# Fixing where VectorE's feed-forward weight sums stand in its queue (two-layer decoder trunk, one core)

## The chip, the cores and the metric

One core of a Trainium2 chip runs the whole program. The time is the device time of one execution in microseconds (us); the time before is 2376.92 us, the median of 3 runs (2371.43 to 2380.17). All instruction times below are read from one profiled execution of the kernel before.

## The reference, cut to what matters

The model is a trunk of two residual layers on 1024 tokens of width 1024. Layer 0 mixes with retention and RWKV-7 heads, layer 1 with sliding-window attention; each is followed by a SwiGLU feed-forward network of width 2816. The change is in the feed-forward networks only:

```python
def swiglu(h, w_gate, w_up, w_down):
    return (jax.nn.silu(h @ w_gate) * (h @ w_up)) @ w_down
...
    h = h + mix
    n = rms_norm(h, norm2_g[layer])
    h = h + swiglu(n, ffn_w_gate[layer], ffn_w_up[layer], ffn_w_down[layer])
return rms_norm(h, final_g)
```

## The kernel before, in words

**Arithmetic.** Activations are kept transposed (128 channels by tokens), the tokens in two halves of 512; `h[0]` and `h[1]` hold the residual of each half in SBUF. A float32 factor is split into a high and a low part, and a product is three matmuls of 128x128 by 128x512 (hi·hi, hi·lo, lo·hi). `prod` (L1172) issues them at L1175, L1176, L1177, so a product over 4 contraction tiles is 12 matmuls into one PSUM bank. The weight is split for each product by `wsplit` (L335 on ScalarE for the high part, L336 mostly on GpSimd for the low part) or by `vsplit` (L1348 and L1349). The split tiles rotate through six buffers.

**Products of blocks.** Instead of eight block products for a 2x2 block matrix, the feed-forward matrices use seven, with sums of weight blocks and of activation blocks (Winograd's form of Strassen's scheme). The weight sums are made on VectorE from weights just loaded, in place as far as possible:
- In the gate and up matrices: `wsums` (L1202) makes four sums (L1208 to L1211) of a pair's four 128x512 blocks; there is one call for gate and one for up. `late_splits` (L1256) is a generator that calls it for every pair of output tiles and loads the next pair's raw weights behind it.
- In the down matrix: `down` (L1378) makes s1 = a21 + a22, W0 = s1 - a11, then a21 = a11 - a21 and later W0 = a12 - W0, all through `vop`, so all have L1375.

**Gate and up.** First come the *early* products (`ffn_early`, L1240): all 11 pairs, two of seven products, each ended by `up` (L1226, VectorE), which multiplies silu(gate) by the up product straight out of PSUM. Then come the *late* pairs (`ffn_pair`, L1284; `late`, L1179): five products a matrix, whose additions into SBUF are L1182. The first late pair's weight sums are asked for before the last early pair, the second's while the first late pair's products are issued. The PSUM banks `ps_m` (two of them) are passed from the last early pair to the first late one: the late product that takes the bank has to wait until `up` has read it.

**Down.** The 11 tiles of the hidden dimension are worked through in groups: two groups of 4 in layer 0 (the rest is done in another way), groups of 4, 4 and 3 in layer 1. In a group there are four pairs of output tiles (`dp` 0 to 3), and for each step a loop over them. Call the banks A[dp] and B[dp]. The steps are: A = a11·X; B = W0·X2, with additions into h[1]; A += a12·X, with additions into h[0]; B += a21·X3, with additions into h[1]; B += a22·X4, with additions into h[0]; then A = s1·X1, each followed by an addition of A[dp] into h[1]; and last A += W0·X6 *into the same four banks*, each followed by a second addition of A[dp] into h[1]. TensorE may start the last step's product into A[dp] only when VectorE has read A[dp] for the first of these two additions. The next group's weights are loaded meanwhile, and nothing in the data ties the next group's sums to these additions.

**What sets the order.** The program is written as one stream; a scheduler, which runs over it with a timeline of its own, decides for each engine in which order its instructions stand. On the chip each engine works strictly in that order and waits on semaphores: an instruction whose operand isn't there holds up all behind it on its engine. `keep_in_program_order` (used by `keep`, L488, on DMAs) fixes some instructions; otherwise the scheduler is free within the data dependencies.

Of the kernel before, what the change touches and what calls it, by code (L numbers as in the profile page):

```python
# [13 lines left out]
ALU = mybir.AluOpType  # L14
# [190 lines left out]
class Kern:  # L205
# [281 lines left out]

    def keep(self, i):  # L488
        return self.tc.keep_in_program_order(i)

    def loads(self):

# [706 lines left out]
        use("12", u1)  # L1199
        yield  # L1200

    def wsums(self, raw, sp):  # L1202

        V = self.nc.vector
        f1, f2 = raw
        a11, a12, a21, a22 = f1[:, :HT], f1[:, HT:], f2[:, :HT], f2[:, HT:]
        s1 = self.t(sp, [P, HT], "ws", 2)
        V.tensor_tensor(out=s1, in0=a21, in1=a22, op=ALU.add)  # L1208
        V.tensor_tensor(out=a21, in0=a11, in1=a21, op=ALU.subtract)
        V.tensor_tensor(out=a11, in0=s1, in1=a11, op=ALU.subtract)  # L1210
        V.tensor_tensor(out=a12, in0=a12, in1=a11, op=ALU.subtract)  # L1211
        v = dict(s1=s1, s2=a11, s3=a21, s4=a12, a22=a22)
        return lambda nm: self.wsplit(v[nm], HT)

    def uses(self, L, p, sp, x=None):

        nc, sg = self.nc, {}
        V, S = nc.vector, nc.scalar

        def gate(nm, c):  # L1220
            sg[nm] = self.t(sp, [P, HT], "sg", 2) if nm == "11" else c
            S.activation(sg[nm], c, AF.Silu)

        def up(nm, c):
            o = x[nm] if x else sg[nm]
            V.tensor_tensor(out=o, in0=sg[nm], in1=c, op=ALU.mult)  # L1226
            d = self.hid[2 * L + int(nm[1]) - 1][2 * p + int(nm[0]) - 1]
            if x and p == NP - 1:
                self.owed.append((d, o))
            else:  # L1230
                nc.sync.dma_start(d, o)

        return gate, up
# [22 lines left out]
    def late_splits(self, L, wp):  # L1256

        def load(p):
            raws = [[self.rawtile(wp) for _ in range(2)] for _ in range(2)]
            for j in range(2):  # L1260
                for i, nm in enumerate(("gate", "up")):
                    self.nc.sync.dma_start(raws[i][j], self.A[f"w_{nm}{L}"][2 * p + j])
            return raws

        nxt = load(0)
        for p in range(NP):
            ws = [self.wsums(r, wp[0]) for r in nxt]
            if p == 0:
                yield
            if p + 1 < NP:  # L1270
                nxt = load(p + 1)
            for nm in ("s2", "s1", "s3", "a22", "s4"):
                for i in range(2):
                    yield ws[i](nm)
# [97 lines left out]
        return self.t(pool, [P, m * P], "ws", bufs)[:, : n * P].rearrange("p (k c) -> p k c", c=P)  # L1372

    def vop(self, o, x, y, f=ALU.add):
        self.nc.vector.tensor_tensor(out=o, in0=x, in1=y, op=f)  # L1375
        return o

    def down(self, L, fp, fz, rest, X=()):  # L1378


        op, S = self.vop, self.nc.scalar
        h0, h1 = (self.kt(self.h[hf]) for hf in range(2))
        dps = range(KT // 2)
        j = len(X)

        def place():
            nonlocal j
            i, j = j % (12 if L else 14), j + 1
            if i >= 8 if L else i < 6:
                return self.t(fp, [P, 2, HT], "ha", 4 if L else 6, F32R)  # L1390
            return self.t(self.pp, [P, 2, HT], "n8", 8, F32R)

        def plain(hf, f):
            return self.plain8(L, hf, f, place(), self.t(fp, [P, HT], "hr", 4))

        for gi, g in enumerate(DGROUPS[L]):
            n, ps = g[1] - g[0], range(*g)
            ta, tb = ("fffy", "mmrc")[:: 1 - 2 * (gi % 2)]
            s1, u0, a1 = [], [], []
            W = [self.wdown(L, 0, g, fp, "wd0", 5)]  # L1400
            X = X or [plain(0, 2 * p) for p in ps]
            W += [self.wdown(L, 2 * i, g, fp, "wd0", 5) for i in (1, 2, 3)]
            for i in dps:
                W[i] += self.wdown(L, 2 * i + 1, g, fp, "wd1", 6 - L)
            A = [self.pst(t, [P, HT]) for t in ta]
            for dp in dps:
                a11, a12, a21, a22 = W[dp]
                self.prod(A[dp], self.vsplit(a11), X, True, False)
                u0.append(self.t(fz, [P, HT], "u0", 4))
                S.copy(u0[dp], A[dp])  # L1410
                s1.append(op(self.wsum(fp, n, 4, 8), a21, a22))
                a1.append(a11)
                W[dp][0] = op(self.wsum(fp, n, 4, 8), s1[dp], a11, ALU.subtract)
            X = [self.sums8(L, p, 2, place()) for p in ps]
            B = [self.pst(t, [P, HT]) for t in tb]
            for dp in dps:
                self.prod(B[dp], self.vsplit(W[dp][0]), X, True, False)
                y = op(self.t(fz, [P, HT], "y", 2), B[dp], u0[dp])
                op(h1(2 * dp), h1(2 * dp), y)
                op(W[dp][2], a1[dp], W[dp][2], ALU.subtract)  # L1420
            X = [plain(0, 2 * p + 1) for p in ps]
            for dp in dps:
                self.prod(A[dp], self.vsplit(W[dp][1]), X, False, True)
                op(h0(2 * dp), h0(2 * dp), A[dp])
                op(W[dp][0], W[dp][1], W[dp][0], ALU.subtract)
            X = [self.sums8(L, p, 3, place()) for p in ps]
            for dp in dps:
                self.prod(B[dp], self.vsplit(W[dp][2]), X, False, False)
                y = op(self.t(fz, [P, HT], "y", 2), B[dp], u0[dp])
                op(h1(2 * dp + 1), h1(2 * dp + 1), y)  # L1430
            X = [self.sums8(L, p, 4, place()) for p in ps]
            while self.owed:
                self.keep(self.nc.sync.dma_start(*self.owed.pop(0)))
            for _ in rest:
                pass
            for dp in dps:
                self.prod(B[dp], self.vsplit(W[dp][3]), X, False, True)
                op(u0[dp], B[dp], u0[dp])
                op(h0(2 * dp + 1), h0(2 * dp + 1), u0[dp])
            X = [self.sums8(L, p, 1, place()) for p in ps]  # L1440
            X6 = [plain(1, 2 * p + 1) for p in ps]
            if g[1] == NP:
                yield
            A = [self.pst(t, [P, HT]) for t in ta]
            for dp in dps:
                self.prod(A[dp], self.vsplit(s1[dp]), X, True, False)
                op(h1(2 * dp + 1), h1(2 * dp + 1), A[dp])
            for dp in dps:
                self.prod(A[dp], self.vsplit(W[dp][0]), X6, False, True)
                op(h1(2 * dp), h1(2 * dp), A[dp])  # L1450
            X = ()
        yield

# [387 lines left out]
```

## Time and profile before

| | us |
|---|---|
| median of 3 runs (lowest, highest) | 2376.92 (2371.43, 2380.17) |
| the profiled execution, whole | 2374.81 |
| its span, first to last instruction | 2373.0 |
| VectorE (DVE) busy in the span | 1667.4 (70%) |
| ScalarE (ACT) busy | 1054.7 (44%) |
| GpSimd (POOL) busy | 948.4 (40%) |
| mean granted clock of TensorE | 0.99 of full speed |

A row of the timeline gives start, duration, engine, line, operation, output<-inputs with shapes, and in brackets how long the engine sat idle before and what released it. PE is TensorE's matmuls, each shown 0.39 us long though the next may start earlier; "PEclk" is the granted share of its clock. Names of tiles are the program's, without numbers: `ws` a weight sum, `wd` a raw down weight, `wq` and some `n` raw gate and up weights, `w` and `wr` split weights, `h` the residual, `ps_..` PSUM banks, `nq` temporaries.

### The profile page before, as it was taken

The numbers are of one execution on the slowest core, as the hardware profiler recorded it, in microseconds if no ns is written. First come the engines' busy times: TensorE is split into PE (matmuls) and PEld (weight loads), VectorE is DVE, ScalarE is ACT, GpSimd is POOL, SyncE is SP. The second block draws the span as 40 slices with busy tenths as digits, with TensorE's granted clock in tenths as the row PEclk, the third lists the DMA queues.
The fourth block names the chain that finished last, engine by engine and source line by source line (L and its number), as shares of the span: only waits on it lengthen the run. The fifth ranks groups of instructions, "written<-read, shape, count | busy, mean of one in ns | idle before, by whom it ended". The sixth has DMA issues, their size and how long they took to land. (4 is left out here: it accounts for less than half of the span.)

```text
span 2373.0 us, 35626 instructions
## 1 busy us (share of the span) xinstructions
PE 2312.1 (97%) x13092; PEld 1828.9 (77%) x13092; DVE 1667.4 (70%) x2630; ACT 1054.7 (44%) x1946; POOL 948.4 (40%) x746
## 2 busy tenths in 40 slices
PE   8999999999999999999999999999999999999997
PEld 6777777777777888888778877777787888877885
DVE  6876865774667358887675668567548778888776
ACT  5354533324456333333333556557645333333335
POOL 3123221201342057776667300002103577767665
PEclk9999999999999999999999999999999999999998
DMA  7555544443445545554554321232236465547652
GB/s 271 203 199 197 176 154 132 128 115 114 148 164 183 208 164 206 211 197 163 218 220 142 123 66 64 71 127 71 100 128 221 170 216 213 209 175 280 245 193 87
DMA packets 167741, 395.92 MB, mean 167 GB/s; under 512 B 42896, under 2 KB 45584, under 8 KB 167568
## 3 DMA queue, kind: packets, MB, share of 16 engines
q1 hardware_dynamic: 164448, 388.15, 47.8%
q10 hardware_dynamic: 2832, 4.45, 0.5%
q8 instruction: 104, 1.70, 0.3%
q0 software_dynamic: 288, 1.05, 0.1%
q14 instruction: 69, 0.57, 0.1%
HBM read 271.29 MB, written 116.92 MB: 164 GB/s over the span
## 5 line engine op out<-in xcount | busy, mean ns | idle before, releaser
L240 PE MATMUL ps_f<-n,w 128*128 128x512 f32 x1440 | 385.6, 415 | 8.6 <-ACT w L335 6.4
L240 PEld LDWEIGHTS ps_f<-n,w 128*128 128x128 f32 x1440 | 268.2, 192 | 93.6 <-issue 24.5
L335 ACT CAST w<-wr 128x512 fp32r<-128x512 f32 x244 | 147.9, 612 | 182.9 <-PE ps_f L352 73.1
L336 POOL TENSOR_TENSOR w<-wr,w 128x512 fp32r<-128x512 f32 x68 | 92.1, 1363 | 280.0 <-ACT w L335 223.0
L336 DVE TENSOR_TENSOR w<-wr,w 128x512 fp32r<-128x512 f32 (+1 forms) x176 | 123.8, 706 | 71.5 <-ACT w L335 71.3
L336 POOL TENSOR_TENSOR w<-wq,w 128x512 fp32r<-128x512 f32 x92 | 130.5, 1431 | 29.2 <-ACT w L335 27.2
L351 PE MATMUL ps_f<-n,w 128*128 128x512 f32 x356 | 141.7, 398 | 0.0
L352 PE MATMUL ps_f<-n,w 128*128 128x512 f32 x356 | 141.0, 396 | 0.6 <-POOL w L336 0.6
L350 PE MATMUL ps_f<-n,w 128*128 128x512 f32 x356 | 140.8, 396 | 0.6 <-ACT n L1601 0.5
L1182 DVE TENSOR_TENSOR nq<-ps_m,u 128x512 f32<-128x512 f32 x88 | 58.8, 685 | 104.3 <-PE ps_m L1177 104.2
L336 POOL TENSOR_TENSOR wx<-wr,wx 128x512 fp32r<-128x512 f32 x8 | 10.6, 1319 | 301.8 <-ACT wx L335 301.6
L1175 PE MATMUL ps_f<-n,w 128*128 128x512 f32 x298 | 118.5, 398 | 4.7 <-DVE h L1375 3.1
L1175 PE MATMUL ps_m<-n,w 128*128 128x512 f32 x300 | 117.5, 392 | 1.5 <-DVE h L1375 1.5
L1176 PE MATMUL ps_f<-n,w 128*128 128x512 f32 x298 | 117.2, 393 | 0.1
L1176 PE MATMUL ps_m<-n,w 128*128 128x512 f32 x300 | 116.8, 389 | 0.0
L1177 PE MATMUL ps_m<-n,w 128*128 128x512 f32 x300 | 116.8, 389 | 0.0
L1177 PE MATMUL ps_f<-n,w 128*128 128x512 f32 x298 | 116.7, 393 | 0.0
L358 POOL TENSOR_TENSOR n<-nq,n 128x512 fp32r<-128x512 f32 x54 | 91.5, 1707 | 8.9 <-ACT n L356 8.9
L1175 PE MATMUL ps_m<-cb,w 128*128 128x512 f32 x240 | 93.4, 389 | 1.0 <-DVE nq L1182 1.0
L1176 PE MATMUL ps_m<-cb,w 128*128 128x512 f32 x240 | 93.4, 389 | 0.0
L1177 PE MATMUL ps_m<-cb,w 128*128 128x512 f32 x240 | 93.4, 389 | 0.0
L1349 POOL TENSOR_TENSOR w<-wd,w 128x512 fp32r<-128x512 f32 (+1 forms) x53 | 76.0, 1444 | 34.8 <-ACT w L1348 34.8
(525 smaller groups left out, 6467.1 us busy)
## 6 DMA issues: line engine op xcount, KB each, us to landing
hc<-n SPq DMA_DIRECT2D x74, 512.0 KB, 2.6
wsp<-w SPq DMA_DIRECT2D x54, 512.0 KB, 3.3
w<-wsp SPq DMA_DIRECT2D x54, 512.0 KB, 3.4
wq<-in_w_gate SPq DMA_DIRECT2D x44, 512.0 KB, 4.3
u<-u SPq DMA_DIRECT2D x88, 256.0 KB, 2.9
n<-hc SPq DMA_DIRECT2D x43, 512.0 KB, 5.5
wr<-in_w_in SPq DMA_DIRECT2D x34, 512.0 KB, 4.8
hid<-n SPq DMA_DIRECT2D x66, 256.0 KB, 2.0
```

What stands on the lines that cost most here:

```text
L240: self.nc.tensor.matmul(out, lhsT, rhs, **kw)
L335: nc.scalar.copy(hi[:, :n], raw[:, c])
L336: self.lo.tensor_tensor(out=lo[:, :n], in0=raw[:, c], in1=hi.bitcast(F32)[:, :n], op=ALU.subtract)
L350: nc.tensor.matmul(ps, hi, rh, start=k == 0, stop=False)
L351: nc.tensor.matmul(ps, hi, rl, start=False, stop=False)
L352: nc.tensor.matmul(ps, lo, rh, start=False, stop=k == n - 1)
L358: e.tensor_tensor(out=lo, in0=src, in1=hi.bitcast(F32), op=ALU.subtract)
L1175: mm(ps, hi, xh, start=first and k == 0, stop=False, skip_group_check=True)
L1176: mm(ps, hi, xl, start=False, stop=False, skip_group_check=True)
L1177: mm(ps, lo, xh, start=False, stop=last and k == len(w) - 1, skip_group_check=True)
L1182: add = lambda o, x, y: V.tensor_tensor(out=o, in0=x, in1=y, op=ALU.add)
L1349: nc.gpsimd.tensor_tensor(out=lo, in0=v, in1=hi.bitcast(F32), op=ALU.subtract)
```

## The change

A helper `behind(i, first)` tells the scheduler that instruction i stands behind instruction `first`. It is an edge for ordering only (NoSync): both are on VectorE, and no semaphore is added.
- In `down`, group g+1's s1[dp] = a21 + a22 stands behind group g's *second* addition of A[dp] into h[1] (the list `ends`). W0 and the in-place difference follow by their data.
- In `late_splits`, for the second late pair the first two sums of gate and of up stand behind the last early pair's multiplication `up`.

```diff
+    def behind(self, i, first):
+        self.tc.add_manual_dep(
+            i.ins, first.ins.name,
+            mybir.DependencyInfo(mybir.DependencyClass.NoSync, mybir.DependencyReason.DATA), reason="behind",
+        )
...
-    def wsums(self, raw, sp):
+    def wsums(self, raw, sp, first=None):
...
-        V.tensor_tensor(out=s1, in0=a21, in1=a22, op=ALU.add)
-        V.tensor_tensor(out=a21, in0=a11, in1=a21, op=ALU.subtract)
+        i = [V.tensor_tensor(out=s1, in0=a21, in1=a22, op=ALU.add)]
+        i.append(V.tensor_tensor(out=a21, in0=a11, in1=a21, op=ALU.subtract))
+        if first is not None:
+            for x in i:
+                self.behind(x, first)
...
-            ws = [self.wsums(r, wp[0]) for r in nxt]
+            ws = [self.wsums(r, wp[0], last if p == 1 else None) for r in nxt]
             if p == 0:
                 yield
+                last = self.last_up
...
                 s1.append(op(self.wsum(fp, n, 4, 8), a21, a22))
+                if ends:
+                    self.behind(self.last_vop, ends[dp])
...
+            ends = []
             for dp in dps:
                 self.prod(A[dp], self.vsplit(W[dp][0]), X6, False, True)
                 op(h1(2 * dp), h1(2 * dp), A[dp])
+                ends.append(self.last_vop)
```

(`last_up` and `last_vop` keep the instruction that `up` and `vop` issued last.) Every engine has the same instructions as before. VectorE's order differs in five places: the second late pair of both layers, and the down groups behind the first (one in layer 0, two in layer 1). TensorE's differs in two short places, ScalarE's in one; the orders of GpSimd and of the DMA queue are the same. Lines below 495 of the kernel before stand 7 to 15 lines further down in the changed kernel (`vop` L1375 is L1386, `late` L1182 is L1189, `wsums` L1208 to L1211 are L1215, L1216, L1220 and L1221, `up` L1226 is L1236).

**Layer 0, down, from the first group to the second (VectorE).** The rows follow the last addition into h[0] of the first group. `h1_..<-h1_..,ps_f_1653` is the addition of A[0] (ps_f_1653, 1654, 1655 and ps_y_1656 are A[0] to A[3] of the last two steps), `ws<-wd1` an s1, `ws<-ws,wd0` a W0, `wd1<-wd0,wd1` the in-place difference of the second group. Before:

```order
L1375 TENSOR_TENSOR ws_1687_11179<-wd1_1677_11150 128x512
L1375 TENSOR_TENSOR h1_1033_6865<-h1_1033_6865,ps_f_1653_10990 128x512
L1375 TENSOR_TENSOR ws_1688_11181<-ws_1687_11179,wd0_1665_11122 128x512
L1375 TENSOR_TENSOR wd1_1677_11150<-wd0_1665_11122,wd1_1677_11150 128x4x128
L1375 TENSOR_TENSOR ws_1691_11200<-wd1_1678_11152 128x512
L1375 TENSOR_TENSOR h1_1033_6865<-h1_1033_6865,ps_f_1654_10991 128x512
L1375 TENSOR_TENSOR ws_1692_11202<-ws_1691_11200,wd0_1674_11144 128x512
L1375 TENSOR_TENSOR ws_1695_11221<-wd1_1679_11154 128x512
L1375 TENSOR_TENSOR wd1_1678_11152<-wd0_1674_11144,wd1_1678_11152 128x4x128
L1375 TENSOR_TENSOR ws_1696_11223<-ws_1695_11221,wd0_1675_11146 128x512
L1375 TENSOR_TENSOR ws_1699_11242<-wd1_1680_11156 128x512
L1375 TENSOR_TENSOR wd1_1679_11154<-wd0_1675_11146,wd1_1679_11154 128x4x128
```

And now:

```order
L1386 TENSOR_TENSOR h1_1033_6865<-h1_1033_6865,ps_f_1653_10990 128x512
L1386 TENSOR_TENSOR h1_1033_6865<-h1_1033_6865,ps_f_1654_10991 128x512
L1386 TENSOR_TENSOR h1_1034_6866<-h1_1034_6866,ps_f_1655_10992 128x512
L1386 TENSOR_TENSOR h1_1034_6866<-h1_1034_6866,ps_y_1656_10993 128x512
L1386 TENSOR_TENSOR h1_1033_6865<-h1_1033_6865,ps_f_1653_10990 128x512
L1386 TENSOR_TENSOR ws_1687_11179<-wd1_1677_11150 128x512
L1386 TENSOR_TENSOR ws_1688_11181<-ws_1687_11179,wd0_1665_11122 128x512
L1386 TENSOR_TENSOR wd1_1677_11150<-wd0_1665_11122,wd1_1677_11150 128x4x128
L358 TENSOR_TENSOR n8_1719_11339<-hr_1720_11340,n8_1719_11339 128x512
L1386 TENSOR_TENSOR h1_1033_6865<-h1_1033_6865,ps_f_1654_10991 128x512
L1386 TENSOR_TENSOR ws_1691_11200<-wd1_1678_11152 128x512
L1386 TENSOR_TENSOR ws_1692_11202<-ws_1691_11200,wd0_1674_11144 128x512
```

Before, one sum stood ahead of the first addition, three between the first and the second, and six between the second and the third (the row behind the last one shown); now the four first additions stand together, and each pair's three sums behind its second addition.

**Layer 1, from the last early pair to the first late one (VectorE).** `sg` is the last early `up`, `wq5`, `wq4` and `n8` are the second late pair's raw weights (gate, then up), `nq<-ps_m_2576` and `nq<-ps_m_2578` are the first late pair's first additions for gate and up. Before:

```order
L1208 TENSOR_TENSOR ws_2596_16467<-wq5_2583_16349 128x512
L1209 TENSOR_TENSOR wq5_2583_16349<-wq4_2582_16348,wq5_2583_16349 128x512
L1210 TENSOR_TENSOR wq4_2582_16348<-ws_2596_16467,wq4_2582_16348 128x512
L1211 TENSOR_TENSOR wq4_2582_16348<-wq4_2582_16348 128x512
L1208 TENSOR_TENSOR ws_2597_16472<-n8_2573_16336 128x512
L1209 TENSOR_TENSOR n8_2573_16336<-n8_2572_16335,n8_2573_16336 128x512
L1226 TENSOR_TENSOR sg_2565_16311<-sg_2565_16311,ps_m_2564_16272 128x512
L1182 TENSOR_TENSOR nq_2580_16346<-ps_m_2576_16342,u0_2574_16338 128x512
L1210 TENSOR_TENSOR n8_2572_16335<-ws_2597_16472,n8_2572_16335 128x512
L1211 TENSOR_TENSOR n8_2572_16335<-n8_2572_16335 128x512
L1182 TENSOR_TENSOR nq_2589_16382<-ps_m_2578_16344,u0_2575_16340 128x512
```

And now:

```order
L1236 TENSOR_TENSOR sg_2565_16311<-sg_2565_16311,ps_m_2564_16272 128x512
L1215 TENSOR_TENSOR ws_2596_16467<-wq5_2583_16349 128x512
L1215 TENSOR_TENSOR ws_2597_16472<-n8_2573_16336 128x512
L1189 TENSOR_TENSOR nq_2580_16346<-ps_m_2576_16342,u0_2574_16338 128x512
L1216 TENSOR_TENSOR wq5_2583_16349<-wq4_2582_16348,wq5_2583_16349 128x512
L1216 TENSOR_TENSOR n8_2573_16336<-n8_2572_16335,n8_2573_16336 128x512
L1220 TENSOR_TENSOR wq4_2582_16348<-ws_2596_16467,wq4_2582_16348 128x512
L1220 TENSOR_TENSOR n8_2572_16335<-ws_2597_16472,n8_2572_16335 128x512
L1221 TENSOR_TENSOR wq4_2582_16348<-wq4_2582_16348 128x512
L1221 TENSOR_TENSOR n8_2572_16335<-n8_2572_16335 128x512
L1189 TENSOR_TENSOR nq_2589_16382<-ps_m_2578_16344,u0_2575_16340 128x512
```

`up` went from behind six of the eight sums to the front, and the up matrix's first addition (`nq_2589`) still stands behind all eight; between them gate's and up's sums now alternate.

On TensorE in the same place two matmuls of the product into ps_c, which stood ahead of the product into ps_m_2578 (the one that takes the bank from `up`), now stand behind it.

More of the change, by code (lines that the diff above doesn't have):

```diff
@@ L1225, in up @@
             o = x[nm] if x else sg[nm]
-            V.tensor_tensor(out=o, in0=sg[nm], in1=c, op=ALU.mult)
+            self.last_up = V.tensor_tensor(out=o, in0=sg[nm], in1=c, op=ALU.mult)
             d = self.hid[2 * L + int(nm[1]) - 1][2 * p + int(nm[0]) - 1]
@@ L1374, in vop @@
     def vop(self, o, x, y, f=ALU.add):
-        self.nc.vector.tensor_tensor(out=o, in0=x, in1=y, op=f)
+        self.last_vop = self.nc.vector.tensor_tensor(out=o, in0=x, in1=y, op=f)
         return o
@@ L1383, in down @@
         dps = range(KT // 2)
-        j = len(X)
+        j, ends = len(X), []
         def place():
```

## The prediction

> **What bounds the kernel now.** I read the page's busy line first, then who TensorE waits for, then the timeline of TensorE and of VectorE around those waits.
>
> ```profile
> PE 2312.1 (97%) x13092; PEld 1828.9 (77%) x13092; DVE 1667.4 (70%) x2630; ACT 1054.7 (44%) x1946; POOL 948.4 (40%) x746
> ```
>
> TensorE is the bound: the feed-forward stages are one stream of matmuls, and only a gap in that stream can be won or lost. The list of TensorE's waits (total, times, longest) names three that VectorE ends in the places of this change, one instance each:
>
> ```profile
> PE ps_f L1175 <- DVE h L1375: 3.1, 1, 3.1
> PE ps_m L1175 <- DVE sg L1226: 2.1, 1, 2.1
> PE ps_m L1175 <- DVE h L1375: 1.5, 1, 1.5
> ```
>
> Call them **B** (layer 0, first to second down group), **C** (layer 1, last early to first late pair) and **E** (layer 1, second to third down group). The other two edited places, **A** (layer 0, late pair) and **D** (layer 1, first to second down group), have no wait here. What VectorE does ahead of B:
>
> ```profile
> 1206.71 1.79 DVE L1375 TENSOR_TENSOR ws<-wd 128x512 f32<-128x512 f32 x1 [1.16 <-POOL w L1349]
> 1208.42 0.67 DVE L1375 TENSOR_TENSOR h<-h,ps_f 128x512 f32<-128x512 f32 x1
> ...
> 1219.94 0.68 DVE L1375 TENSOR_TENSOR h<-h,ps_f 128x512 f32<-128x512 f32 x1
> ...
> 1224.01 0.67 DVE L1375 TENSOR_TENSOR h<-h,ps_f 128x512 f32<-128x512 f32 x1
> ...
> 1236.08 0.69 DVE L1375 TENSOR_TENSOR ws<-wd,ws 128x512 f32<-128x512 f32 x1 [2.02 <-POOL wr L1349]
> 1241.74 0.69 DVE L1375 TENSOR_TENSOR y<-ps_f,u 128x512 f32<-128x512 f32 x1 [4.96 <-PE ps_f L1177]
> ```
>
> The third first-addition, for which TensorE waits, runs at 1219.94 because six sums of the next group stand between it and the second one. The sums are early: when all are done, at 1236.77, VectorE idles 4.96 us until the first product that uses one has ended. A sum with both inputs in SBUF takes 0.67 us or up to 1.8; an addition out of PSUM stays at 0.68.
>
> **The change, part by part.** *B.* TensorE's rows at the wait:
>
> ```profile
> 1217.27 0.39 PE L1177 MATMUL ps_f<-n,w 128*128 128x512 f32 x1
> 1220.76 0.47 PE L1175 MATMUL ps_f<-n,w 128*128 128x512 f32 x1 [3.10 <-DVE h L1375]
> ...
> 1221.53 0.62 PE L1175 MATMUL ps_f<-n,w 128*128 128x512 f32 x1
> ...
> 1224.94 0.40 PE L1177 MATMUL ps_f<-n,w 128*128 128x512 f32 x1
> ```
>
> Undisturbed, a product of 12 matmuls takes 2.72 us, the distance of these two products' first matmuls, so 0.227 a matmul:
>
> ```profile
> 1212.06 0.39 PE L1175 MATMUL ps_f<-n,wr 128*128 128x512 f32 x1
> ...
> 1214.78 0.39 PE L1175 MATMUL ps_f<-n,w 128*128 128x512 f32 x1
> ```
>
> From 1217.27 to 1224.94 there are 12 steps in 7.67 us instead of 2.72: 4.95 us lost, 3.26 of them the gap itself and 1.69 a stretch in which matmuls follow each other at 0.43 us. The table of stretches shows why (the column behind the busy times is the granted clock); its four rows are B, C, a place of layer 1 that isn't edited, and E:
>
> ```profile
> 1221.50:1224.90 3.40, 3.40 (x9) 2.63 (x8) 3.19 (x6) 0.00 (x0) 0.00 (x0) 0.50 0.00 0
> 1839.30:1842.80 3.50, 3.50 (x9) 2.73 (x10) 1.76 (x3) 0.00 (x0) 0.41 (x1) 0.51 0.77 241
> 2136.30:2139.70 3.40, 3.18 (x8) 2.51 (x9) 3.19 (x3) 0.00 (x0) 3.40 (x3) 0.50 1.01 412
> 2280.50:2283.00 2.50, 1.04 (x5) 0.86 (x5) 2.50 (x5) 0.51 (x1) 1.00 (x1) 1.00 0.97 348
> ```
>
> Behind the gaps of B and C the clock is halved for 3.4 us; behind E's shorter one it isn't. With the change the four first additions have nothing in front of them, so gap and slow stretch both go: **-4.95**.
>
> Is the cover enough for the sums that now start later? They start behind the second addition of A[0], whose product ends at about 1214.78 + 0.39 = 1215.1, not at 1206.71. Up to the last W0 stand 15 instructions with SBUF inputs and 4 additions. From 1206.71 to 1224.01 VectorE ran 19 instructions without idling, 13 of the first kind and 6 additions: 17.9 us, less 6 x 0.60, is 1.10 each. So W0[3] is ready at 1215.1 + 4 x 0.6 + 15 x 1.10 = 1234.0, and split by 1236.1, with the durations of a split's two halves:
>
> ```profile
> 1234.06 0.62 ACT L1348 CAST wr<-ws 128x512 fp32r<-128x512 f32 x1
> ```
>
> ```profile
> 1837.99 1.72 POOL L336 TENSOR_TENSOR wr<-wq,wr 128x512 fp32r<-128x512 f32 x1
> 1844.56 1.29 POOL L336 TENSOR_TENSOR wr<-wq,wr 128x512 fp32r<-128x512 f32 x1 [4.85 <-ACT wr L335]
> ```
>
> TensorE wants it after four X6 products, four a11 products and three W0 products from 1212.06: 1212.06 + 11 x 2.72 = 1242.0. That leaves 5.9 us. Behind ScalarE's cast for W0[3] stand copies and later casts, which then move by less than this slack. Cost: nothing; the cover is the a11 products.
>
> *C.* The same count:
>
> ```profile
> 1836.77 0.39 PE L1176 MATMUL ps_c<-n,w 128*128 128x512 f32 x1
> 1839.22 0.71 PE L1175 MATMUL ps_m<-n,wr 128*128 128x512 f32 x1 [2.07 <-DVE sg L1226]
> ...
> 1842.72 0.42 PE L1177 MATMUL ps_m<-n,wr 128*128 128x512 f32 x1
> ```
>
> 9 steps in 5.95 us instead of 2.04: 3.91 lost, 2.22 by the gap and 1.69 by the clock. VectorE there:
>
> ```profile
> 1829.41 0.69 DVE L1208 TENSOR_TENSOR ws<-wq 128x512 f32<-128x512 f32 x1
> ...
> 1835.12 1.77 DVE L1208 TENSOR_TENSOR ws<-n 128x512 f32<-128x512 f32 x1
> ...
> 1838.50 0.67 DVE L1226 TENSOR_TENSOR sg<-sg,ps_m 128x512 f32<-128x512 f32 x1
> 1839.09 0.68 DVE L1182 TENSOR_TENSOR nq<-ps_m,u 128x512 f32<-128x512 f32 x1
> ```
>
> `up` moves from 1838.50 to before the sums: **-3.91**. But up's first addition now has the sums close in front of it. The second sum needs the raw up weights, which were there at 1835.12 at the latest. From there: that sum, gate's addition, six sums, then the addition. GpSimd is busy until 1837.99 + 1.72 = 1839.7 and then idle until 1844.56, so I take 1.7 for the sums begun before 1839.7 and 0.6 behind: 1836.8, 1837.4, 1839.1, 1840.2, four more to 1842.6, done at 1843.3. TensorE wants that bank for its next product 26 steps after 1836.77, at 1842.66. A new wait of about 0.6 at most if the weights came then, none if earlier: I take **+0.5**. With every sum at 1.78 it would be 1848.9, a wait of 6.2.
>
> Here a rule speaks otherwise. The Trainium skill, page "TensorE: Matmul & The Clock Gate", section "Why this matters for your kernels", says that gaps of TensorE above about 3 us bring the half clock. By it C's 2.07 us would cost no slow stretch, and the sum below would be 1.7 us smaller. The trace shows clock 0.51 behind C, so the measurement decides and I give that sum no share of the chance.
>
> *E.* Here VectorE is held up by a sum whose weights have not landed, with the additions queued behind it:
>
> ```profile
> 2270.39 1.53 DVE L1375 TENSOR_TENSOR ws<-wd 128x384 f32<-128x384 f32 x1 [2.72 <-DMA wd<-in_w_down]
> ...
> 2281.19 0.67 DVE L1375 TENSOR_TENSOR h<-h,ps_m 128x512 f32<-128x512 f32 x1
> ```
>
> ```profile
> 2280.16 0.39 PE L1177 MATMUL ps_c<-n,w 128*128 128x512 f32 x1
> ...
> 2282.01 0.47 PE L1175 MATMUL ps_m<-n,w 128*128 128x512 f32 x1 [1.46 <-DVE h L1375]
> ```
>
> The distance is 1.85 instead of 0.23 and the clock stays at 1.00: **-1.62**. Behind the edge the DMA wait falls in time in which VectorE has no other work due.
>
> *A and D.* No wait goes. In A six sums come between `up` and gate's first addition:
>
> ```profile
> 846.59 0.68 DVE L1226 TENSOR_TENSOR sg<-sg,ps_m 128x512 f32<-128x512 f32 x1
> ...
> 849.31 1.28 DVE L1182 TENSOR_TENSOR nq<-ps_m,u 128x512 f32<-128x512 f32 x2
> ```
>
> ```profile
> 854.03 0.39 PE L1175 MATMUL ps_m<-cb,w 128*128 128x512 f32 x1
> ```
>
> The four instructions from 846.59 on took 2.72 us, 0.68 each. So the addition would end at 847.2 + 6 x 0.68 + 0.69 = 852.0, and TensorE takes the bank at 854.03: 0, with 2.0 us of cover. At 1.78 a sum it would be 858.6, a wait of 4.6. D is B again with no gap to win: 0. The two matmuls that TensorE does later in C, and the other short exchanges on TensorE and ScalarE, move no work: 0. The DMA queue keeps its order, so a load is issued earlier just as its buffer comes free earlier.
>
> *Sum.* -4.95 - 3.91 - 1.62 + 0.5 = **-10.0 us**. Against the profiled execution's own 2374.81 (span 2373.0 and 1.8 around it) that is 2364.8. The median shown is 2.1 us above that execution, so I forecast 2366.9 for the median, 0.4% less. About 0.5% (12 us) is what a measurement of this kernel can tell from no change, so the likeliest class is "within 0.5%" although I expect a gain.
>
> **The rivals.** Times are on the scale of the median.
> 1. *A new wait takes the place of the old one* at C (or A). If GpSimd's splits fall beside all the sums, C's addition is 6.2 us late and the clock drops again, 7.9 in all: -10.5 + 7.9 = -2.6, so 2374.3. For it: sums of 1.7 us stand there now. Against it: GpSimd's 4.85 us of idling.
> 2. *The slow side: the sums come too late for their own products* in B, D and E. At 1.78 us each, W0[3] is ready at 1215.1 + 2.4 + 26.7 = 1244.2, split at 1246.3, 4.3 late, plus 1.69 of slow clock: 6.0 a group. Three groups are +18.0 against -10.5: 2384.4. It decides from a mean of 1.50 us a sum ((1242.0 - 2.1 - 2.4 - 1215.1) / 15). The trace's mean is 1.10, in the same mixture.
> 3. *The half clock falls elsewhere.* The slow stretches are 3.4 us long and don't scale with the gap. The third row of stretches belongs to this wait, of 1.82 us, while E's 1.46 brought none:
>
> ```profile
> 2136.52 0.79 PE L1177 MATMUL ps_f<-n,wr 128*128 128x512 f32 x1 [1.82 <-POOL wr L1349]
> ```
>
> If the later program is 9 us earlier, that one may vanish, or one or two may come at other short waits: -1.7 or up to +3.4, so 2365.2 or 2370.3. The same page of the Trainium skill, section "What's actually happening", says that activity is judged in windows of 3.4 us that run freely; the trace's lengths agree.
> 4. *The saving is given back*, because a load behind B or C isn't ready sooner, or the edges do nothing: 2376.9. Against it: no wait of TensorE on a DMA is in the list in these stages.
>
> **How the numbers follow.** Forecast 60%, rival 1 10%, rival 2 6%, rival 3 16%, rival 4 8%. The range should hold the forecast with a few us of scatter (the three runs of before lie 8.7 apart, which is five slow stretches), rival 3 and rival 1: 2359 to 2375. Outside stay rivals 2 and 4 and some scatter, about 18%. Faster by over 0.5% is below 2365.0: a third of the forecast's share and half of rival 3's, 0.28. Slower by over 0.5% is above 2388.8: part of rival 2 and scatter, 0.05. The rest, 0.67, is within.
>
> **What would show it.** Right: the three wait rows are gone from TensorE's list, the clock is 1.00 in B and C, and the first additions run within a microsecond of their product's end. A short wait of a product on a late addition (L1189 in the changed kernel) in C confirms the +0.5. Wrong: waits of ScalarE on the sums of a down group followed by waits of TensorE on split weights (rival 2), a wait above 2 us in C (rival 1), or all three rows gone and the span unchanged (rival 4).

## The result, and the profile after

The changed kernel takes 2367.81 us (median of 6 runs, 2365.26 to 2370.77); the kernel before, beside it, 2376.51 (6 runs). The ratio is 0.9961, with a 95% interval of 0.9949 to 0.9974: 9 us faster, give or take 3. The forecast was 2366.9 and "within 0.5%"; so it came.

The profiled execution took 2369.26 us (span 2367.5). TensorE is still the bound, with a share as before (busy line of the page, changed kernel):

```profile
PE 2308.0 (97%) x13092; PEld 1826.0 (77%) x13092; DVE 1660.7 (70%) x2630; ACT 1055.3 (45%) x1946; POOL 953.9 (40%) x746
```

In the list of what TensorE waited for (total, times, longest) the three rows of B, C and E are gone. New against the list of before is the length of the first row below, a product that waits for a late pair's addition (L1189): 2.7 us in two instances, where before there was one of 1.0, in layer 0. The second row, a wait near 2132, stood in the list of before as well. The third has grown from 0.8 to 1.6; it is long in just those profiles of this study in which the place near 2132 ran at full clock, so what TensorE doesn't lose there it waits for 14 us later. Neither is touched by the change:

```profile
PE ps_m L1182 <- DVE nq L1189: 2.7, 2, 1.8
PE ps_f L1184 <- POOL wr L1360: 2.4, 2, 1.8
PE ps_r L1182 <- ACT wr L1359: 1.6, 2, 1.4
```

**B.** VectorE in the changed kernel: the four first additions, then the first second addition (1218.21), and behind it the sums; the last row is W0[3]. The first of them runs 1.4 us behind the end of its product, after other additions, but nothing waits for it yet; the other three run right behind theirs.

```profile
1208.70 0.67 DVE L1386 TENSOR_TENSOR h<-h,ps_f 128x512 f32<-128x512 f32 x1
1210.05 0.69 DVE L1386 TENSOR_TENSOR h<-h,ps_f 128x512 f32<-128x512 f32 x1 [0.68 <-PE ps_f L1184]
1212.77 0.69 DVE L1386 TENSOR_TENSOR h<-h,ps_f 128x512 f32<-128x512 f32 x1 [2.03 <-PE ps_f L1184]
1215.49 0.69 DVE L1386 TENSOR_TENSOR h<-h,ps_y 128x512 f32<-128x512 f32 x1 [2.03 <-PE ps_y L1184]
1218.21 0.69 DVE L1386 TENSOR_TENSOR h<-h,ps_f 128x512 f32<-128x512 f32 x1 [2.03 <-PE ps_f L1184]
...
1236.06 0.68 DVE L1386 TENSOR_TENSOR ws<-ws,wd 128x512 f32<-128x512 f32 x1
```

VectorE now idles 2.03 us ahead of each of the last three additions, released by TensorE: the waiting has changed sides. TensorE in the same group, the first matmuls of the last step's products into A[0], A[1] and A[2], and that of the first product that uses W0[3]:

```profile
1215.29 0.39 PE L1182 MATMUL ps_f<-n,wr 128*128 128x512 f32 x1
...
1218.01 0.39 PE L1182 MATMUL ps_f<-n,w 128*128 128x512 f32 x1
...
1220.73 0.39 PE L1182 MATMUL ps_f<-n,w 128*128 128x512 f32 x1
...
1245.21 0.39 PE L1182 MATMUL ps_y<-ha,wr 128*128 128x512 f32 x1
```

The first three stand 2.72 us apart, without a gap. The table of stretches has no idle time and full clock there (the last column but two), and the same at E:

```profile
1220.00:1225.00 5.00, 5.00 (x23) 4.14 (x23) 5.00 (x4) 2.82 (x5) 4.65 (x4) 1.00 0.22 84
...
2274.00:2280.00 6.00, 6.00 (x28) 4.95 (x27) 1.94 (x4) 1.21 (x3) 2.32 (x3) 1.00 0.71 252
```

The product into A[0] began at 1215.29, 3.23 us later than before (1212.06), by work ahead of the edited places in which these two executions differ; that into A[2] at 1220.73, level with 1220.76 before; and the slow stretch behind it is missing.

**E.** The sum whose weights land late no longer stands in front of the additions (VectorE, changed kernel):

```profile
2270.91 0.69 DVE L1386 TENSOR_TENSOR h<-h,ps_m 128x512 f32<-128x512 f32 x1 [2.03 <-PE ps_m L1184]
...
2279.67 0.55 DVE L1386 TENSOR_TENSOR ws<-wd 128x384 f32<-128x384 f32 x1
```

The first sum at 2279.67 waits for no DMA, the additions only for TensorE.

**C.** Here a wait went and another came. VectorE, then GpSimd, then TensorE:

```profile
1829.29 0.69 DVE L1236 TENSOR_TENSOR sg<-sg,ps_m 128x512 f32<-128x512 f32 x1 [1.77 <-PE ps_m L1184]
...
1832.31 1.26 DVE L1215 TENSOR_TENSOR ws<-n 128x512 f32<-128x512 f32 x1 [1.68 <-DMA n<-in_w_up]
...
1837.49 0.68 DVE L1220 TENSOR_TENSOR n<-ws,n 128x512 f32<-128x512 f32 x1
1838.09 1.77 DVE L1221 TENSOR_TENSOR wq<-wq 128x512 f32<-128x512 f32 x1
1839.79 1.76 DVE L1221 TENSOR_TENSOR n<-n 128x512 f32<-128x512 f32 x1
1841.47 1.28 DVE L1189 TENSOR_TENSOR nq<-ps_m,u 128x512 f32<-128x512 f32 x2
```

```profile
1837.87 1.45 POOL L336 TENSOR_TENSOR wr<-wq,wr 128x512 fp32r<-128x512 f32 x1 [1.46 <-ACT wr L335]
1839.28 1.73 POOL L336 TENSOR_TENSOR w<-wq,w 128x512 fp32r<-128x512 f32 x1
```

```profile
1840.14 0.39 PE L1184 MATMUL ps_m<-cb,w 128*128 128x512 f32 x1
1842.30 0.47 PE L1182 MATMUL ps_m<-cb,w 128*128 128x512 f32 x1 [1.77 <-DVE nq L1189]
```

`up` runs at once. But the up matrix's first addition, the first of the two at 1841.47, stands behind all eight sums, and the last two of these run beside GpSimd's splits and take 1.77 us. TensorE goes on 2.16 us behind the matmul at 1840.14, where 0.23 is its step: 1.93 lost, 2.05 by the time its steps are regular again.

The edge also won something that is not among the three rows. Shortly ahead of C's gap TensorE had stood still for the low part of a split weight (before):

```profile
1833.00 0.50 PE L1177 MATMUL ps_r<-n,wr 128*128 128x512 f32 x1 [0.25 <-POOL wr L336]
```

Before, GpSimd made that part beside the sums, in 1.74 us (from 1831.21); now it stands almost alone and takes 1.30 (from 1828.77). TensorE's wait is gone, and with the slower steps behind it 0.55 us: a matmul ahead of it stands 1.75 us earlier than before (1830.62 against 1832.37), one behind it 2.30 (1832.43 against 1834.73).

### The profile page after: what moved, and what is told of

Its sections match the earlier page's. It is cut to its first block, busy times and chain, and to the rows that moved or that the text cites. A ratio compares the mean times of both kernels' runs of the same rounds, so it can differ in the third digit from the quotient of the medians.

```text
span 2367.5 us, 35611 instructions
## 1 busy us (share of the span) xinstructions
PE 2308.0 (97%) x13092; PEld 1826.0 (77%) x13092; DVE 1660.7 (70%) x2630; ACT 1055.3 (45%) x1946; POOL 953.9 (40%) x746
## 4 chain that ended last, share of the span: by engine, by line
PE 76%; DVE 8%; issue 5%; DMA 4%; ACT 3%; POOL 2%; SPq 1%; ACTq 0%; DVEq 0%; POOLq 0%
PE ps_f L240 8%; PE ps_m L1182 7%; PE ps_m L1184 7%; PE ps_m L1183 7%; PE ps_m L240 5%; PE ps_f L352 5%; PE ps_f L351 5%; PE ps_f L350 5%; PE ps_f L1183 4%; PE ps_f L1184 4%; PE ps_f L1182 4%; PE ps_c L1184 2%; PE ps_r L1183 2%; PE ps_r L1184 2%; PE ps_c L1183 2%
## 5 line engine op out<-in xcount | busy, mean ns | idle before, releaser
L1189 DVE TENSOR_TENSOR nq<-ps_m,u 128x512 f32<-128x512 f32 x88 | 58.7, 684 | 97.6 <-PE ps_m L1184 97.5
L1182 PE MATMUL ps_f<-n,w 128*128 128x512 f32 x298 | 117.7, 395 | 1.6 <-ACT u L1337 1.6
L1182 PE MATMUL ps_m<-n,w 128*128 128x512 f32 x300 | 117.4, 392 | 0.0
L1182 PE MATMUL ps_m<-cb,w 128*128 128x512 f32 x240 | 93.5, 390 | 2.7 <-DVE nq L1189 2.7
```

Of the source, the lines that this page charges most:

```text
L1182: mm(ps, hi, xh, start=first and k == 0, stop=False, skip_group_check=True)
L1189: add = lambda o, x, y: V.tensor_tensor(out=o, in0=x, in1=y, op=ALU.add)
```

## The experiments

All ratios are to the kernel before on the same chip; 0.001 is 2.4 us. Each of B, C and E is read in the traces too, since the intervals are 2 to 4 us to either side. Four theories stood behind the expectations. **Theory 1**: the gain is the sum of local gaps that TensorE no longer has, less C's new wait. **Theory 2**: the late edge makes the larger part. **Theory 3**: half-clock stretches that fall by chance make most of the difference, and the new wait eats what C wins. **Theory 4**, on the clock alone: half clock follows a window of fixed length in which TensorE was idle too long.

**The changed kernel once more.**

> The changed kernel itself once more, beside the next ones. Theory 1 (local gaps): B loses its 4.9 us, E its 1.6, and the new wait of 1.8 us at C stands again, so about -8 us against the kernel before, ratio 0.9966, and 1 to 2 us faster than with the down edges alone (-6.7). What is not fixed is the half clock behind C's new wait. Theory 3 (chance makes most of it): -4 us or less.

It came to 0.9966 (0.9952 to 0.9981), so -8.1 us. C's new wait is there again, 1.7 us, with no half clock behind it. Theory 3's 4 us or less lies outside the interval. In the profile of this run a half-clock stretch near 1499 us, outside the edited places, takes 1.3 us back; the first profile of the changed kernel has none there. The two timings together carry a gain of 8 to 9 us.

**Down edges alone.**

```diff
-            ws = [self.wsums(r, wp[0], last if p == 1 else None) for r in nxt]
+            ws = [self.wsums(r, wp[0], None) for r in nxt]
```

> Only the down groups' edges are kept; the second late pair's sums stand as in the kernel before. Theory 1 (the gain is the sum of local gaps: TensorE gets a bank back earlier): the gaps of B and E go, the gap of C (2.1 us, with or without the half clock behind it, 1.7) stays, and no new wait comes at C. B gives -4.9, E -1.6, in all -6.5 us against the kernel before, ratio about 0.9973. Theory 2 (the late edge makes the larger part, the down edges shift only idle time): within 1 us of the kernel before. Theory 3 (half-clock stretches that fall by chance make most of the difference of 9 us between the two kernels): B's shift in the trace is the gap alone, -3.3, and the times differ by less than 5 us from before.

0.9974 (0.9965 to 0.9983): -6.2 us, as theory 1 had it; theory 2 would be at 1.0. Theory 3's "less than 5" lies inside the interval (4.0 to 8.3), and the trace decides against it: TensorE begins the product into A[0] 0.25 us later than before (1212.31 against 1212.06) and the last matmul of that into A[2] 4.70 earlier (1220.24 against 1224.94), so B's shift is 4.95 and not 3.3. Of the three waits only C's is left in TensorE's list:

```profile
PE ps_m L1182 <- DVE sg L1236: 2.0, 1, 2.0
```

**The late edge alone.**

```diff
-                if ends:
-                    self.behind(self.last_vop, ends[dp])
```

> Only the second late pair's edge is kept; the down groups' sums stand as before. Theory 1: the waits of B (3.1 us, and half clock behind it) and E (1.5 us) stay; C loses its gap of 2.1 us and the slow stretch (together -3.9) and gets the new wait of 1.8 us on the up matrix's first addition: net about -2 us against the kernel before, ratio about 0.999. Theory 2 (the late edge makes the larger part): -6 us or more. Theory 3 (the new wait at C eats the whole gain whenever the clock is not halved there): 0 within 1 us.

0.9997 (0.9988 to 1.0006): nothing that can be measured. The trace says why (TensorE's waits; TensorE at C; a stretch behind it; VectorE):

```profile
PE ps_m L1182 <- DVE nq L1189: 4.3, 2, 3.3
```

```profile
1841.16 0.39 PE L1184 MATMUL ps_m<-cb,w 128*128 128x512 f32 x1
1844.89 0.56 PE L1182 MATMUL ps_m<-cb,w 128*128 128x512 f32 x1 [3.34 <-DVE nq L1189]
```

```profile
1845.10:1848.50 3.40, 3.40 (x9) 2.63 (x9) 0.93 (x2) 0.63 (x1) 0.00 (x0) 0.50 0.14 55
```

```profile
1839.00 1.78 DVE L1220 TENSOR_TENSOR n<-ws,n 128x512 f32<-128x512 f32 x1
```

The new wait is 3.34 us here, because a sum that took 0.68 in the changed kernel takes 1.78 and the sums of the up weights begin half a microsecond later against TensorE's work; and it brings the half clock. Lost are 3.73 - 0.23 = 3.50 and about 1.7, against 4.5 gained (the gap, its half clock and the 0.55 us ahead of it): in this execution the edge gives back all that it wins. This is rival 1 of the prediction. Theory 1 had the sign and not the size of the wait; theory 2 falls. Theory 3 had the number, 0 within 1 us, but the gain was eaten by a longer wait with a half clock of its own, not because the old gap had none.

**Four sums behind the up matrix's first addition.**

```diff
-        add(u1, b, u0)
+        self.last_u1 = add(u1, b, u0)
...
-        V.tensor_tensor(out=a11, in0=s1, in1=a11, op=ALU.subtract)
-        V.tensor_tensor(out=a12, in0=a12, in1=a11, op=ALU.subtract)
+        i = [V.tensor_tensor(out=a11, in0=s1, in1=a11, op=ALU.subtract)]
+        i.append(V.tensor_tensor(out=a12, in0=a12, in1=a11, op=ALU.subtract))
+        if first is not None:
+            for x in i:
+                self.behind(x, self.last_u1)
```

> The changed kernel, with the third and the fourth sums of the second late pair (gate and up, four instructions) also put behind the up matrix's first addition, which then has four sums in front of it instead of eight. Theory 1 (C's new wait of 1.8 us comes from the two sums of 1.77 us that stand last in front of that addition, slow because GpSimd's splits run beside them): the wait goes, -1.8 us against the changed kernel, -11 against the one before, and no new wait on the split weights of the second pair. Rival (the queue is held by the landing of the raw up weights, for which VectorE idles 1.7 us in the changed kernel, and then also holds the addition): a wait of 1 us or more stays on the addition.

0.9972 (0.9961 to 0.9984), no faster than the changed kernel. Neither expectation was right: that addition is in time (VectorE idles 0.69 us ahead of it, for its product), but the four sums behind it make the next addition late, and TensorE waits 1.0 us for that one:

```profile
1835.29 0.69 DVE L1189 TENSOR_TENSOR nq<-ps_m,u 128x512 f32<-128x512 f32 x1 [0.69 <-PE ps_m L1184]
...
1836.50 1.78 DVE L1220 TENSOR_TENSOR n<-ws,n 128x512 f32<-128x512 f32 x1
...
1839.90 1.77 DVE L1221 TENSOR_TENSOR n<-n 128x512 f32<-128x512 f32 x1
1841.59 0.68 DVE L1189 TENSOR_TENSOR nq<-ps_m,u 128x512 f32<-128x512 f32 x1
```

**All eight sums behind it.** As above, with the first two sums of gate and up behind `last_u1` as well:

```diff
-                self.behind(x, first)
+                self.behind(x, self.last_u1)
```

> The changed kernel, with all eight sums of the second late pair behind the up matrix's first addition, so that the addition waits for nothing but its product. Theory 1: no wait of TensorE on VectorE is left at C, -1.9 us against the changed kernel, as with half of the sums behind, or the same. Rival (the second pair's split weights then come too late, since the eight sums at up to 1.77 us take some 10 us more before ScalarE and GpSimd can split them): a wait of TensorE on split weights of 1 us or more in the second late pair, and no gain, or a loss of up to 3 us against the changed kernel.

0.9973 (0.9964 to 0.9982). Two additions are late now, by 1.2 and 0.7 us in TensorE's list:

```profile
PE ps_m L1182 <- DVE nq L1189: 2.1, 2, 1.2
...
PE ps_r L1182 <- DVE nq L1189: 0.7, 1, 0.7
```

The wait for C goes to wherever a block of sums stands. The split weights did not come later for it: the longest wait for one, 1.4 us on ScalarE's, is in the changed kernel's list too.

**The sums spread, two at most in front of an addition.**

```diff
-        add(u2, b, u0)
+        self.last_u2 = add(u2, b, u0)
...
-        V.tensor_tensor(out=a11, in0=s1, in1=a11, op=ALU.subtract)
-        V.tensor_tensor(out=a12, in0=a12, in1=a11, op=ALU.subtract)
+        i = V.tensor_tensor(out=a11, in0=s1, in1=a11, op=ALU.subtract)
+        j = V.tensor_tensor(out=a12, in0=a12, in1=a11, op=ALU.subtract)
+        if first is not None:
+            self.behind(i, self.last_u1)
+            self.behind(j, self.last_u2)
```

(`last_u1` as above.)

> The changed kernel with the second late pair's sums spread: the third sums of gate and up behind the up matrix's first addition, the fourth sums behind its second one, so that never more than two sums stand in front of an addition. Theory 1 (each addition can be preceded by two sums of up to 1.78 us in the 2.7 us and more between two products' ends, four or eight are too many): no wait of TensorE on an addition above 0.3 us at C, -1.8 us against the changed kernel (-1 against the variant with four sums behind the addition), and no wait on split weights of the second pair. Rival (the eight sums beside GpSimd's splits, about 11 us, make VectorE late wherever they stand, since three additions come close together there): the wait of about 1 us comes again, at a later addition.

> The variant with the second late pair's sums spread, once more, to see whether it is faster than the changed kernel. Theory 1 (the new wait of 1.8 us at C is all that the changed kernel still loses there): B -4.9, C -3.9, E -1.6, in all -10.4 us against the kernel before, ratio 0.9956; the changed kernel stood at 0.9961 and 0.9966. Rival (the first timing of this variant was lucky, the place of the sums makes no difference): 0.9966 or more.

0.9950 (0.9931 to 0.9968) and 0.9964 (0.9950 to 0.9978). In both traces C has no wait left; the one of 0.9 us that remains in TensorE's list is layer 0's of before:

```profile
PE ps_m L1182 <- DVE nq L1189: 0.9, 1, 0.9
```

The mechanism is theory 1's. The second timing lies nearer to the rival's 0.9966 than to theory 1's 0.9956. That this variant beats the changed kernel (0.9961, 0.9966) is what both traces and both medians (2365.46 and 2367.26 against 2367.81 and 2369.18) point to, but the intervals overlap: it is the best of the versions tried, by some 2 us that the timing alone doesn't prove. Both are faster than the kernel before.

**No splits beside the sums.**

```diff
-            self.lo.tensor_tensor(out=lo[:, :n], in0=raw[:, c], in1=hi.bitcast(F32)[:, :n], op=ALU.subtract)
+            if hi_only:
+                lo = hi
+            else:
+                self.lo.tensor_tensor(out=lo[:, :n], in0=raw[:, c], in1=hi.bitcast(F32)[:, :n], op=ALU.subtract)
```

(`hi_only` is set for the first late pair.)

> The changed kernel with GpSimd's part of the first late pair's weight splits left out (the low part is not computed, the high part is used in its place, so the first late pair's products are other numbers; VectorE, ScalarE and TensorE issue as many instructions as before). Theory 1 (the sums of 1.77 us are slow because GpSimd's splits run beside them): in layer 1 all eight sums of the second late pair take 0.7 us each instead of 1.2 to 1.8, and TensorE's wait of 1.8 us on the up matrix's first addition is gone. Rival (the sums are slow by themselves, in place on tiles just loaded): durations of 1.2 to 1.8 us and the wait stay.

All eight sums take 0.68 or 0.69 us, and TensorE's list has no wait at C. The last sum, and the addition behind, which again waits for its product:

```profile
1831.43 0.69 DVE L1224 TENSOR_TENSOR n<-n 128x512 f32<-128x512 f32 x1
1832.51 0.69 DVE L1192 TENSOR_TENSOR nq<-ps_m,u 128x512 f32<-128x512 f32 x1 [0.39 <-PE ps_m L1187]
```

The same instructions on the same tiles, so GpSimd's work beside them is what makes them slow. (This kernel does less work and computes other numbers, so its one execution, 2362.60 us, can't be set beside the other times.) The Trainium skill, page "SBUF — State Buffer", section "Who interferes with whom", says that a VectorE instruction with two SBUF inputs contends with a GpSimd instruction that reads SBUF, and one with at most one SBUF input, outside the two-port modes, does not; the trace agrees: 0.69 against 1.77 us for the sums, 0.68 for an addition out of PSUM in either case.

**Down sums later still.**

```diff
-                    self.behind(self.last_vop, ends[dp])
+                    self.behind(self.last_vop, ends[-1])
```

> The changed kernel with every s1 of a down group behind the second addition of A[3] instead of its own A[dp], so that the group's sums start up to 8 us later (about 1226.5 in layer 0 instead of 1218.8). It tries how much cover the a11 products give. Theory 1 (VectorE's sums there mostly take 0.7 to 1.1 us; the last W0 is ready near 1242 and split near 1244, needed near 1245): no wait, or up to 1 us in a group; within 2 us of the changed kernel. Rival (the sums come too late for their own products, as with 1.78 us a sum: the last W0 ready at 1226.5 + 15 x 1.78 = 1253, split at 1255): waits of TensorE on split weights of some 8 us in each of the three places, +20 us or more.

The ratio is 0.9975 (0.9963 to 0.9987), 2 to 3 us above the two timings of the changed kernel, with intervals that overlap. The trace gives no reason for a difference in the edited places: from 1100 us on TensorE's list is that of the changed kernel, with no wait in B, D or E. In layer 0 the first sum, W0[3], GpSimd's half of its split, and TensorE's first use of it:

```profile
1225.45 0.68 DVE L1386 TENSOR_TENSOR ws<-wd 128x512 f32<-128x512 f32 x1
...
1236.16 0.68 DVE L1386 TENSOR_TENSOR ws<-ws,wd 128x512 f32<-128x512 f32 x1
```

```profile
1237.63 1.57 POOL L1360 TENSOR_TENSOR wr<-ws,wr 128x512 fp32r<-128x512 f32 x1 [1.94 <-ACT wr L1359]
```

```profile
1243.27 0.39 PE L1182 MATMUL ps_y<-ha,wr 128*128 128x512 f32 x1
```

The 13 sums from 1225.45 to 1236.84 took 0.88 us each, and from the end of the split, 1239.20, 4.1 us of cover are left, even with the sums 6.6 us later than in the changed kernel (1225.45 against 1218.82). Rival 2 falls.

**The kernel before, at other offsets of the clock's windows.**

> The kernel before once more, for the half clock behind its gaps. Theory 4 (activity is judged in windows of 3.41 us that run freely from an offset that differs from run to run; a window in which TensorE idles more than about 1.9 us is followed by one at half clock): the slow stretches start at whole multiples of 3.413 us from one another; B's gap (3.3 us in all) is followed by one nearly always, C's (2.2) and the one of 1.8 us near 2132 only where the window's edge doesn't cut them, and E's (1.6) never. Rival (the length of the gap alone decides, as in the first profile): B, C and the one near 2132 are each followed by half clock again, whatever the offset.

> The same as the run ahead of it, at another offset. Theory 4: where a gap of 1.8 or 2.2 us is cut by a window's edge so that less than about 1.9 us fall into each part, no half clock follows. Rival: the three places are halved as in the first profile.

The two executions took 2374.99 and 2373.51 us. The slow stretches of the first profile (their rows stand in the prediction) begin at 1221.5, 1839.3 and 2136.3: 181 and 87 times 3.413 us apart. In the second profile two begin here, 268 times 3.413 apart, and none behind C:

```profile
1222.80:1226.20 3.40, 3.40 (x8) 2.66 (x9) 3.40 (x6) 0.00 (x0) 0.32 (x1) 0.50 0.00 0
1837.20:1840.60 3.40, 2.00 (x9) 1.31 (x7) 3.31 (x4) 0.62 (x1) 3.40 (x3) 1.00 0.00 0
1840.60:1844.00 3.40, 2.74 (x12) 2.28 (x13) 2.50 (x5) 0.00 (x0) 1.14 (x1) 1.00 0.55 170
...
2137.60:2141.00 3.40, 3.40 (x10) 2.62 (x9) 3.30 (x3) 0.00 (x0) 3.40 (x3) 0.50 1.03 417
```

From 1222.8 on, 180 windows end at 1837.1, the next at 1840.6: C's gap (1838.8 to 1841.3 here) is cut by this edge. The windows keep 2.00 and 2.74 us of busy time (first figure behind the comma), and the clock stays full. In the third profile B's stretch begins at 1220.3, an edge lies 181 windows on at 1838.1, and C's gap is cut again:

```profile
1220.30:1223.70 3.40, 3.40 (x9) 2.62 (x10) 3.40 (x6) 0.00 (x0) 0.28 (x1) 0.51 0.00 0
1834.80:1838.20 3.40, 2.71 (x12) 1.88 (x10) 3.31 (x3) 0.62 (x1) 3.40 (x3) 1.00 0.08 28
1838.20:1841.60 3.40, 2.06 (x9) 1.72 (x10) 3.18 (x5) 0.00 (x0) 1.83 (x2) 1.00 0.35 114
```

In the first profile, for comparison, C's gap lay in one window, and so did two shorter ones, near 2132 and at E:

```profile
1835.90:1839.30 3.40, 1.33 (x7) 0.79 (x5) 3.31 (x4) 0.39 (x1) 3.40 (x3) 1.00 0.00 0
...
2132.90:2136.30 3.40, 1.67 (x7) 0.73 (x5) 2.31 (x3) 2.57 (x5) 2.82 (x2) 1.00 0.42 105
...
2279.70:2283.10 3.40, 1.94 (x9) 1.33 (x8) 3.40 (x7) 0.51 (x1) 1.07 (x2) 1.00 0.93 327
```

Windows with 1.33 and 1.67 us of busy time were followed by half clock, those with 1.94 and more were not. Theory 4's account holds, though its figure of 1.9 us of idling is too high (3.41 - 1.67 = 1.74 was enough); its rival falls: C's gap of the same length, about 2.05 us by the list, was followed by half clock in the first profile and not in these two.

The limit isn't sharp, though. With all eight sums behind the addition, the slow stretch that begins at 2147.3 puts an edge five windows earlier, at 2130.25, and the window from there holds the gap near 2132 as far as the profile can tell. It has less work than the 1.67 above, and yet full clock follows:

```profile
2130.30:2133.70 3.40, 1.62 (x7) 1.36 (x8) 3.26 (x3) 0.73 (x2) 3.40 (x4) 1.00 0.95 325
2133.70:2137.10 3.40, 3.40 (x17) 2.82 (x16) 3.30 (x3) 0.59 (x1) 3.40 (x3) 1.00 1.03 416
```

Over all windows of the thirteen profiles between 1100 and 2330 us, laid out from each one's slow stretches, those with less than 1.55 us of work were all followed by half clock and those with 1.75 or more never; between the two both happened.

## Why the prediction was right, point by point

- **The bound.** Right: only gaps of TensorE counted, and what was won is what the three rows of its list held and a fourth, shorter wait, less one that came.
- **B, -4.95.** Right. In the two executions the product into A[0] stood 3.23 us later than before and that into A[2] 0.03 earlier: 3.26, the gap as predicted; and the stretch behind it is at full clock, 1.69. The cover was there: shifted by these 3.2 us the working had W0[3] ready at 1237.2 and wanted at 1245.2; it was ready at 1236.74 and used from 1245.21.
- **E, -1.62.** Right: no gap, full clock. Together with B it is the -6.57 that the down edges alone should give; they gave -6.2 (2.1 to either side). The size is one of the larger ones: where the first profile waits 1.5 us at E, the two others of the kernel before wait 1.4 and 0.7 (the latter put down to a split weight) and that with the late edge alone 0.6.
- **C, -3.91.** The gap of 2.22 went, as predicted, and with it 0.55 that the working didn't have, the short wait for GpSimd ahead of it. The 1.69 for the clock was right for the profiled execution, and too much for the median: C's gap had half clock behind it in that profile and in the one with the down edges alone, not in the other two of the kernel before. Half of 1.69 is a fairer term.
- **C, the new wait, +0.5: the step that failed.** The mechanism was the one named (up's first addition behind eight sums); the size was 2.05 (1.93 at the wait itself), and 3.50 with half clock where the late edge stood alone. The sums were priced too low, for two reasons. First, the working broke its own rule: the sum begun at 1839.1 should have taken 1.7 and ended at 1840.8, not at 1840.2, which makes the wait 1.2 instead of 0.6. Second, it took the sums begun behind 1839.7 at 0.6 us, because GpSimd idled from there to 1844.56 in the trace of before. That idling went with the gap. GpSimd waits there for ScalarE's high part, and ScalarE for a product of TensorE: 7.57 us before, 3.17 in the changed kernel. With the down edges alone, where C's gap stays, GpSimd idles nearly as long as before (4.52 against 4.85); in the changed kernel it idles 1.46, and its next split comes at 1837.87 (row above), beside the last two sums. The upper end kept for the range, 6.2, was the right thing to keep.
- **A, 0.** Right in the result, by less than thought. The six sums between `up` and gate's first addition took 5.9 us (847.19 to 853.08) instead of 4.1, two of them 1.77 long: the same under-sized term, hidden there by the 2.0 us of cover (in this execution 3.2 more, since TensorE came later), and no wait is in the list. D: 0, right.
- **The sum.** The same matmuls of the two profiled executions, set side by side, give what each place is worth. Ahead of B the changed kernel is 3.23 us later, behind it 1.72 earlier (1223.22 against 1224.94); ahead of C 1.75 earlier, behind its new wait 4.18 (1847.86 against 1852.04); ahead of E 4.24 (2275.92 against 2280.16), behind it 5.94 (2277.06 against 2283.00). That is -4.95, -2.43 and -1.70, in all -9.1 us, or -8.2 with half of the clock's 1.69 at C. Measured were -9.3 and -8.1, each 3 or more to either side. That the forecast of -10.0 met the median so closely is partly luck: two sizes were wrong on the gaining side (the new wait and C's half clock), and the 0.55 us that was left out made up for part of it. The two profiled executions differ by 5.55 us only, since the one of after had come 3.2 us later to B.
- **The rivals.** 1 took place as a mechanism, at a quarter of its price in the changed kernel (2.05 of 7.9), and as a full exchange with the late edge alone. 2 and 4 fell. 3 is real: which short gaps are followed by half clock differs from execution to execution.

## What to carry to other kernels

When an engine's work is moved, don't take another engine's idle time from the trace of before as cover: ask first whether that idling was caused by the very gap that is removed. In an engine that serves a bound engine in order, independent work is best spread in pieces that fit between two due times; a block of it moved elsewhere moves the wait along. And where half clock follows short gaps, price it by how likely the gap falls into one window, not by one profile.

## What the runs showed of the hardware

- A VectorE sum with both inputs in SBUF takes 0.68 us alone and 1.77 beside GpSimd's splits; these take 1.29 alone and 1.73 beside it. An addition with one input in PSUM stays at 0.68.
- The half clock comes in stretches of 3.41 us, whose starts lie whole multiples of 3.413 us apart within an execution (181, 87 and 268 of them) and elsewhere in the next execution. What decides is how much TensorE works in the window of that length ahead of the stretch: less than 1.55 us always brought the half clock in these profiles, 1.75 or more never, and between them it came or not. About half a window of idling is enough, and no single gap needs to be that of a whole window. The Trainium skill, page "TensorE: Matmul & The Clock Gate", section "Why this matters for your kernels", puts the limit at gaps of about 3 us; here gaps of 1.8 and 2.1 us brought it, in some executions and not in others.
